# Hybrid decoder step in float32: how the first output tiles, the loads of x, the small loads and the output are ordered

## The chip, the cores and the metric

The kernel runs on one core of a Trainium2 chip. The metric is the device time of one execution in microseconds (us), lower is better. Three executions of the kernel before took 1625.08, 1626.22 and 1627.49 us; the median is 1626.22 us.

## The reference

One trunk layer of a hybrid decoder over 320 tokens (256 of a prompt and 8 sequences of 8), with 2048 channels, all in float32:

```python
hn = rms_norm(x, lp['norm_mix'])
proj = hn @ lp['w_in']                       # 2048 -> 6656 = 52 tiles of 128 columns
p_rw, p_hg, p_lru = jnp.split(proj, (RWKV_COLS, RWKV_COLS + HGRN_COLS), axis=-1)
y_rw, ... = rwkv7_mix(p_rw, ...)             # 12 heads of 64, delta rule
y_hg, ... = hgrn2_mix(p_hg, ...)             # 6 heads, 128 x 128 state
y_lru, ... = rglru_mix(p_lru, ...)           # 512 channels
x = x + concat([y_rw, y_hg, y_lru]) @ lp['w_out']
hn = rms_norm(x, lp['norm_ffn'])
gte, val = jnp.split(hn @ lp['ffn_w_up'], 2, axis=-1)
gc, ... = causal_dwconv(gte, ...)
x = x + (silu(gc) * val) @ lp['ffn_w_down']  # d_ff = 5632
```

After it stands a final RMSNorm. Outputs are the two parts of y and all recurrent states.

## The kernel before, in words

Activations lie transposed: 16 row blocks of 128 channels by 320 tokens. To keep float32 accuracy, TensorE multiplies split operands. ScalarE rounds a weight chunk to a high part `wh` (L173) and VectorE subtracts to get the low part `wl` (L174); x is split likewise into `xh` and `xl` (L217, L218), already scaled by the norm's weights `nmix`. An output tile of 128 columns then takes 16 row blocks times three products (`wh·xh`, `wh·xl`, `wl·xh`), 48 matmuls with 320 columns each. The RMS factor `rstd` is applied after the product, when VectorE evicts the accumulator.

Weights come in chunks of eight row blocks (128 x 1024 floats, 512 KB), so an input tile has two chunks. The order of all chunks stands in the list `chunks` (L97 on). SP issues their loads. `prefetch` (L176) keeps at most four chunks loaded and two split ahead of the one in use. There are three buffers each for `raw`, `wh` and `wl`.

**The first stage (L256 to L317).** Three products of a zero tile (`idle`, L260) run while the first loads are under way. In four groups g of four row blocks, SP is given half a chunk of tile 0, four loads of x of 160 KB each (L278) and half a chunk of tile 1; ScalarE and VectorE split them in that order. The squares of x for the norm are computed on ScalarE and added on VectorE into `ssq` beside that. `nmix` has its own small load on ScalarE's queue (L263), and `prm` and `cst` are loaded from there in groups 1 and 2. GpSimd issues the small loads `shift`, `h0` and `ccv` (L322 to L326) at the start. `first_tiles` (L300) multiplies, for each g, four row blocks of tile 0 and then of tile 1, into two PSUM banks of `aux_r`.

**The front (L395 to L418).** Then the third tile (k of head pair 0, `ps_k`) runs through `gemm` (L189), which takes one of two accumulators (`acc`). After it stands the product of `ones` with `ssq` (L401), which gives the sum of squares; ScalarE takes the root (L234) and VectorE the reciprocal (L235). The masks are loaded (L405) behind other work on SP's queue. Tiles 0 and 1 are evicted by `shifted` (L372), which also needs `shift`; they become `lora` and `sg`, the inputs of the low-rank products of every RWKV pair.

**The mixing stage (L1187 to L1198)** goes through `ORDER`: pair 0 of RWKV, HGRN head 0, pair 1, head 1 and so on, then the gated recurrences. A pair has tiles k, r, v; a head q, f, v, g. In `rwkv_pair(0, ps_k)` the tiles r and v are computed, v into a bank of `aux_r`. So the accumulators go to k, r, then q of head 0 and f of head 0, in turn.

The recurrences' own instructions are put between the tiles by a planner written in Python. `state["clock"]` counts 0.136 for every matmul of a tile (`GEMM_COST`) and 0.4 for every step of a recurrence (`AUX_COST`). Each of six queues (`QUEUES`, one for RWKV operands "f", one for RWKV chunks "r", and so on) holds jobs, one of which is active at a time. A step that ends in `yield w` is due again when the clock has gone on by w. `tick` runs what is due; it is called after every 4 row blocks of the `wh` products and at the end of a chunk, so three times per chunk. For pair 0, `rwkv_operands` (L474) yields `L_FIRST` before its first products (L482, the low-rank products with `lora`); after them come the square of k (L499) and its product (L502). `rwkv_chunks` (L563) waits for v and the operands. Its job for pair 1 begins when that of pair 0 has ended. A pair ends in `rwkv_norm` with L842 and L844. `y_steps` (L1176) splits the mixed outputs in turn once all six pairs are done; the output projection starts when eight of them are split (L1198), and reads x again (L1207).

**The end (L1281 to L1292).** After the last tile of the MLP's down projection, the sum of squares, a root and a reciprocal, VectorE scales 16 tiles one after the other (L1289, L1291), and each is stored by a DMA of its own, in turn on SP's and ScalarE's queues.

The order of instructions within an engine is otherwise chosen at build time by the framework's scheduler; `tc.keep_in_program_order` holds an instruction at its place in the text. `behind` (L185) is such a load on SP.

Of the kernel before, what the change touches and what calls it, by code (L numbers as in the profile page):

```python
# [66 lines left out]
def kernel(ctx: ExitStack, tc: tile.TileContext, i: dict, o: dict):  # L67
# [30 lines left out]
    for h in range(2):  # L98
        for n in range(2):
            chunks.append((i["w_in"][n, h], 8))  # L100
    for n in [c for k, m in ORDER for c in
                       {"r": (3 + 3 * m, 2 + 3 * m, 4 + 3 * m), "h": range(20 + 4 * m, 24 + 4 * m),
                        "l": (44 + 4 * m, 46 + 4 * m, 45 + 4 * m, 47 + 4 * m)}[k]]:
        for h in range(2):
            chunks.append((i["w_in"][n, h], 8))
# [83 lines left out]
    def gemm(pieces, xh, xl, k0=0, first=True, last=True, ps=None):  # L189
        if ps is None:  # L190
            ps = acc_p.tile([P, 512], F32, tag="acc", name="acc")
        for c, kc in enumerate(pieces):
            prefetch()
            wh, wl = splits.pop(state["used"])
            state["used"] += 1
            for k in range(kc):
                st = first and c == 0 and k == 0
                PE.matmul(ps[:, :T], wh[:, k, :], xh[k0 + k], start=st, stop=False)  # L198
                PE.matmul(ps[:, :T], wh[:, k, :], xl[k0 + k], start=False, stop=False)  # L199
                state["clock"] += 2 * GEMM_COST  # L200
                if k % 4 == 3:
                    tick()
            for k in range(kc):
                en = last and c == len(pieces) - 1 and k == kc - 1
                PE.matmul(ps[:, :T], wl[:, k, :], xh[k0 + k], start=False, stop=en)  # L205
# [77 lines left out]
    for g in range(4):  # L283
        ks = slice(4 * g % 8, 4 * g % 8 + 4)
        split_weights(2 * (g // 2), ks)
# [5 lines left out]
        split_weights(2 * (g // 2) + 1, ks)  # L291
        if g:
            squares(range(4 * g - 4, 4 * g) if g < 3 else ())
        if g == 1:
            tc.keep_in_program_order(S.dma_start(out=prm, in_=i["prm"]))
        if g == 2:
            tc.keep_in_program_order(S.dma_start(out=cst, in_=i["cst"]))
    state["raw"] = state["split"] = 4

    def first_tiles():  # L300

        pss = [aux_r(), aux_r()]
        for g in range(4):
            for n, ps in enumerate(pss):
                wh, wl = splits[2 * (g // 2) + n]
                for k in range(4 * g, 4 * g + 4):
                    PE.matmul(ps[:, :T], wh[:, k % 8, :], xh[k], start=(k == 0), stop=False)
                    PE.matmul(ps[:, :T], wh[:, k % 8, :], xl[k], start=False, stop=False)
                for k in range(4 * g, 4 * g + 4):
                    PE.matmul(ps[:, :T], wl[:, k % 8, :], xh[k], start=False, stop=(k == NK - 1))  # L310
            state["clock"] += 24 * GEMM_COST
            if g % 2:
                for n in range(2):
# [81 lines left out]
    def rwkv_front():  # L395
        ps_0, ps_1 = first_tiles()
# [4 lines left out]
        tc.keep_in_program_order(PE.matmul(ps_n[:, :T], ones, ssq, start=True, stop=True))  # L401
# [16 lines left out]
        return ps_k  # L418
# [41 lines left out]
    def rwkv_pair(p, ps_k=None):  # L460
# [5 lines left out]
        for name, n in (("k", 3), ("r", 2), ("v", 4)):  # L466
            ps = gemm(W_CHUNKS, xh, xl, ps=aux_r()) if p == 0 and name == "v" else ps_k
            ps_k = None
# [5 lines left out]
    def rwkv_operands(p, lw, box):  # L474
# [6 lines left out]
        for n, ps in enumerate((ps_w, ps_a)):  # L481
            PE.matmul(ps[:, :T], lw[half[n], n, :], lora[half[n], :], start=True, stop=True)  # L482
# [338 lines left out]
    def rwkv_norm(p, lw, y, bo):  # L821
# [21 lines left out]
        yo = yp.tile([P, T], F32, tag=f"y{p}", name="yo")  # L843
# [33 lines left out]
    def hgrn_steps(n, box):  # L877
# [148 lines left out]
        yo = yp.tile([P, T], F32, tag=f"y{NPAIR + n}", name="yo")  # L1026
# [77 lines left out]
    def lru_steps(m, box):  # L1104
        tiles = (2 * m, 2 * m + 1)
        rs, ths, aes = [], [], []
        for n, (xc, _) in zip(tiles, box["x"]):
            w = rp.tile([P, 2, P], F32, tag="wg", name="wg", bufs=1)
            G.dma_start(out=w, in_=i["wg"][n])
# [35 lines left out]
        for j, (n, hs) in enumerate(zip(tiles, rs)):  # L1145
# [4 lines left out]
            yo = yp.tile([P, T], F32, tag=f"y{NPAIR + NHG + n}", name="yo")  # L1150
# [36 lines left out]
    ps_k = rwkv_front()  # L1187
    spawn("y", y_steps())
    for kind, n in ORDER:
# [4 lines left out]
        if (kind, n) == ("r", 0):  # L1194
            rwkv_pair(0, ps_k)
# [9 lines left out]
    def x2_tile(n, ps):  # L1205
        t = yp.tile([P, T], F32, tag=f"y{n}", name="x2")
        G.dma_start(out=t, in_=i["xT"][n])  # L1207
# [78 lines left out]
    for n in range(NK):  # L1286
# [5 lines left out]
        (S if n % 2 else SY).dma_start(out=o["yT"][n], in_=y)  # L1292
# [5 lines left out]
L_FIRST = 11.0  # L1298
# [23 lines left out]
NFIRST = 4  # L1322
QUEUES = "nrfhly"
# [3 lines left out]
    "yT": (NK, P, T), "p_rwkv": (NPAIR, P, 64), "s_rwkv": (NPAIR, P, SB, 64), "nshift": (P, 20, 9),  # L1327
# [141 lines left out]
```

## Time and profile before

| what | value |
|---|---|
| median of three executions | 1626.22 us |
| the profiled execution | 1627.56 us |
| its span on the chip | 1625.8 us |
| busy share of PE / DVE / ACT / POOL | 99% / 60% / 50% / 9% |
| bytes moved by DMA | 238.91 MB, 147 GB/s on the mean |

In the profile, PE is TensorE, DVE VectorE, ACT ScalarE and POOL GpSimd; SP only issues DMAs. A row of the timeline gives the start and the duration in us, the engine, the line, the operation, the tiles (out<-in), the shape, a count, and in brackets how long the engine had been idle before and what released it. A matmul's duration overlaps with its neighbour's, so the rate is read from the starts. A row of the windows view gives, for a stretch of the span, its length, then for each engine the busy time and in brackets the number of instructions, then the granted TensorE clock, the DMA engines' busy share and GB/s.

### The profile page before, as it was taken

What the parts mean: (1) busy time and instruction counts of PE and PEld (TensorE: products, weight loads), DVE (VectorE), ACT (ScalarE), POOL (GpSimd) and SP (SyncE); (2) the same over time, 40 slices, a digit from 0 to 9 for tenths busy, and PEclk for the clock granted to TensorE, in tenths of its full rate; (3) what the DMA queues carried; (4) which work ended last, traced back from release to release, by engine and by line L of the source; (5) the groups of instructions that cost most, each with busy time, mean ns of one, the idle gap of its engine ahead of it and who ended that gap; (6) DMA issues with size and microseconds to landing.
All of it is one profiled execution on the core that took longest, in us unless ns stands there. A gap on an engine that the chain in (4) does not pass through costs nothing.

```text
span 1625.8 us, 29013 instructions
## 1 busy us (share of the span) xinstructions
PE 1601.6 (99%) x11478; PEld 1548.6 (95%) x11478; DVE 973.9 (60%) x1965; ACT 809.6 (50%) x1280; POOL 144.7 (9%) x364
## 2 busy tenths in 40 slices
PE   9999999999999999999999999999999999999996
PEld 8888989898989999999999999999999999999996
DVE  7786878777776765555555554343455555554444
ACT  7766766676766964443434343323334343344442
POOL 2101111111111300001111110000011110000000
PEclk9999999999999999999999999999999999999998
DMA  8444343444344554454445444555444444445553
GB/s 266 154 132 135 117 141 120 128 120 136 114 135 122 168 169 150 151 158 148 151 148 156 145 153 144 147 152 149 155 151 154 146 153 145 155 146 156 149 151 109
DMA packets 87791, 238.91 MB, mean 147 GB/s; under 512 B 16712, under 2 KB 31096, under 8 KB 87656
## 3 DMA queue, kind: packets, MB, share of 16 engines
q1 hardware_dynamic: 81496, 221.01, 44.4%
q0 software_dynamic: 4576, 14.16, 2.6%
q8 instruction: 90, 1.47, 0.4%
q10 hardware_dynamic: 1584, 1.89, 0.3%
q14 instruction: 45, 0.37, 0.1%
HBM read 225.66 MB, written 11.37 MB: 146 GB/s over the span
## 4 chain that ended last, share of the span: by engine, by line
PE 85%; ACT 7%; DVE 4%; DMA 2%; issue 2%; SPq 0%; POOL 0%; DVEq 0%; ACTq 0%
PE acc L198 26%; PE acc L205 26%; PE acc L199 26%; DVE wl L174 1%; PE aux_r L703 1%; PE aux_h L914 1%; ACT wh L173 1%; DMA raw<-in_w_in 1%; ACT L935 0%; ACT L893 0%; ACT L1023 0%; DVE x L1289 0%; PE aux_r L656 0%; PE aux_r L729 0%; DMA mskf<-in_msk 0%
## 5 line engine op out<-in xcount | busy, mean ns | idle before, releaser
L173 ACT CAST wh<-raw 128x1024 fp32r<-128x1024 f32 (+2 forms) x412 | 421.6, 1025 | 542.8 <-PE acc L199 338.2
L198 PE MATMUL acc<-xh,wh 128*128 128x320 f32 x2192 | 661.0, 315 | 0.0
L199 PE MATMUL acc<-xl,wh 128*128 128x320 f32 x2192 | 648.2, 309 | 0.0
L174 DVE TENSOR_TENSOR wl<-raw,wh 128x1024 fp32r<-128x1024 f32 (+2 forms) x412 | 489.9, 1190 | 224.5 <-ACT wh L173 113.1
L198 PEld LDWEIGHTS acc<-xh,wh 128*128 128x128 f32 x2192 | 411.7, 188 | 13.6 <-issue 10.7
L199 PEld LDWEIGHTS acc<-xl,wh 128*128 128x128 f32 x2192 | 411.7, 188 | 1.3
L205 PE MATMUL acc<-xh,wl 128*128 128x320 f32 x2192 | 372.6, 312 | 0.0
L205 PEld LDWEIGHTS acc<-xh,wl 128*128 128x128 f32 x2192 | 332.3, 188 | 2.8
L198 PE MATMUL acc<-hh,wh 128*128 128x320 f32 x704 | 207.9, 308 | 0.0
L199 PE MATMUL acc<-hl,wh 128*128 128x320 f32 x704 | 207.9, 308 | 0.0
L199 PEld LDWEIGHTS acc<-hl,wh 128*128 128x128 f32 x704 | 132.1, 188 | 0.0
L198 PEld LDWEIGHTS acc<-hh,wh 128*128 128x128 f32 x704 | 131.7, 187 | 0.0
L205 PE MATMUL acc<-hh,wl 128*128 128x320 f32 x704 | 118.8, 308 | 0.0
L1251 POOL COPY ncch<-fe 128x18 f32<-128x18 f32 x44 | 49.7, 1131 | 652.7 <-DVE fe L1250 652.7
L205 PEld LDWEIGHTS acc<-hh,wl 128*128 128x128 f32 x704 | 107.1, 187 | 0.0
L1261 DVE TENSOR_TENSOR fv<-acc,rstd 128x320 f32<-128x320 f32 x44 | 21.6, 492 | 98.5 <-PE acc L205 98.5
L1249 DVE TENSOR_TENSOR fe<-acc,rstd 128x256 f32<-128x256 f32 x44 | 18.7, 425 | 99.6 <-PE acc L205 99.6
L214 ACT CAST hh<-fv 128x320 fp32r<-128x320 f32 x44 | 20.3, 460 | 96.9 <-DVE fv L1263 96.9
L198 PE MATMUL acc<-yhl,wh 128*128 128x320 f32 x224 | 66.2, 310 | 0.0
L199 PE MATMUL acc<-yhl,wh 128*128 128x320 f32 x224 | 66.0, 307 | 0.0
L1256 DVE SCALAR_TENSOR_TENSOR fc<-fe,prm,fc 128x336 f32<-128x336 f32 x88 | 49.8, 566 | 1.6
L1254 ACT ACTIVATE fc<-fe,prm 128x336 f32<-128x336 f32 x44 | 29.4, 669 | 35.7 <-DVE fe L1250 35.7
(416 smaller groups left out, 1616.6 us busy)
## 6 DMA issues: line engine op xcount, KB each, us to landing
raw<-in_w_up SPq DMA_DIRECT2D x176, 512.0 KB, 3.5
raw<-in_w_in SPq DMA_DIRECT2D x100, 512.0 KB, 3.5
raw<-in_w_dn SPq DMA_DIRECT2D x64, 512.0 KB, 3.4
raw<-in_w_out SPq DMA_DIRECT2D x32, 512.0 KB, 3.6
raw<-in_w_dn SPq DMA_DIRECT2D x32, 384.0 KB, 3.0
out_s_hgrn<-hs POOLq DMA_DIRECT2D x12, 256.0 KB, 4.6
xr<-in_xT SPq DMA_DIRECT2D x16, 160.0 KB, 3.8
hs<-in_hs POOLq DMA_DIRECT2D x10, 256.0 KB, 4.2
```

The lines of the kernel that those rows point to most:

```text
L173: S.copy(wh[:, ks, :], raws[n][:, ks, :])
L174: V.tensor_tensor(wl[:, ks, :], raws[n][:, ks, :], wh[:, ks, :].bitcast(F32), op=ALU.subtract)
L198: PE.matmul(ps[:, :T], wh[:, k, :], xh[k0 + k], start=st, stop=False)
L199: PE.matmul(ps[:, :T], wh[:, k, :], xl[k0 + k], start=False, stop=False)
L205: PE.matmul(ps[:, :T], wl[:, k, :], xh[k0 + k], start=False, stop=en)
L214: S.copy(xh, src)
L703: PE.matmul(ps[q, b * 64:(b + 1) * 64], lhs[q, b, q], r[q], start=True, stop=True)
L1249: V.tensor_tensor(e[:, 2:258], ps[:, 0:TP], rstd[:, 0:TP], op=ALU.mult)
L1251: G.tensor_copy(ncch[:, j], e[:, 248:EX].rearrange("p (b s) -> p b s", s=10)[:, :, 8:10])
L1254: S.activation(c[:, 0:N], e[:, 0:N], AF.Identity, scale=pc("fw", 3 * j), bias=pc("fb", j))
L1256: V.scalar_tensor_tensor(c[:, 0:N], e[:, m:m + N], pc("fw", 3 * j + m), c[:, 0:N], op0=ALU.mult, op1=ALU.add)
L1261: V.tensor_tensor(val, ps[:, :T], rstd, op=ALU.mult)
```

## The change

Six edits:

- The first stage computes three tiles in turn instead of two: tiles 0, 1 and 3 (`FIRST_TILES`; tile 3 is k of pair 0). For each group of four row blocks, tile 0, 1 and 3 get 12 matmuls each. k goes into an accumulator. In the mixing stage's order, tile 3 is left out of `chunks`.
- After the first two matmuls of tile 0, two zero products (`NIDLE2`) are issued on TensorE.
- x is loaded in pairs of row blocks (320 KB); row block 0 comes together with `nmix` in one load `x0`, row block 1 in a load of its own. All row blocks lie in one tile `yall`, which is also where the mixed outputs, the second residual and the final output lie.
- Small loads move: `shift`, `h0`, `ccv` and the first `wg` from GpSimd's queue to SP's, at later places; `cst` and `prm` behind all splits of the first stage, still on ScalarE's queue.
- The front computes r of pair 0 before `rwkv_pair(0)` is entered, and the product with `ssq` stands within r's last chunk, ahead of its `wl` products. The low-rank products of pair 0 are held at their place, and `L_FIRST` goes from 11 to 15.
- The output is stored in pairs of tiles, eight DMAs of 320 KB in turn on SP's and ScalarE's queues.

```diff
     for h in range(2):
-        for n in range(2):
+        for n in FIRST_TILES:
             chunks.append((i["w_in"][n, h], 8))
...
-    def gemm(pieces, xh, xl, k0=0, first=True, last=True, ps=None):
+    def gemm(pieces, xh, xl, k0=0, first=True, last=True, ps=None, within=None):
...
+            if within and c == len(pieces) - 1:
+                within()
             for k in range(kc):
                 en = last and c == len(pieces) - 1 and k == kc - 1
                 PE.matmul(ps[:, :T], wl[:, k, :], xh[k0 + k], start=False, stop=en)
...
-    nmix = cp.tile([P, NK], F32, tag="nmix", name="nmix")
-    S.dma_start(out=nmix, in_=i["prm"][:, PRM["nmix"]:PRM["nmix"] + NK])
-    xh, xl, xr = [], [], []
+
+    x0 = et("diff", NK + T)
+    nmix = x0[:, 0:NK]
+    yall = yp.tile([P, NK, T], F32, tag="yall", name="yall")
+    xh, xl = [], []
...
-    raws[3] = rp.tile([P, 10, P], F32, tag="big", name="raw3", bufs=BB)
+    NF = len(FIRST_TILES)
+    for n in (NF, NF + 1):
+        raws[n] = rp.tile([P, 10, P], F32, tag="big", name=f"raw{n}", bufs=BB)
     for g in range(4):
         ks = slice(4 * g % 8, 4 * g % 8 + 4)
-        if g < 3:
-            load(2 * (g // 2), ks)
-        for k in range(4 * g, 4 * g + 4):
-            t = yp.tile([P, T], F32, tag=f"y{k}", name="xr")
-            SY.dma_start(out=t, in_=i["xT"][k])
-            xr.append(t)
-        if g == 3:
-            load(2, ks)
-        load(2 * (g // 2) + 1, ks)
+        first = NF * (g // 2)
+        load(first, ks)
+        if g == 0:
+            SY.dma_start(out=x0, in_=i["x0"])
+            SY.dma_start(out=yall[:, 1, :], in_=i["xP"][0, :, 1, :])
+        for m in range(2 * g, 2 * g + 2):
+            if m:
+                SY.dma_start(out=yall[:, 2 * m:2 * m + 2, :], in_=i["xP"][m])
+        for n in range(1, NF):
+            load(first + n, ks)
...
-        split_weights(2 * (g // 2) + 1, ks)
-        if g:
-            squares(range(4 * g - 4, 4 * g) if g < 3 else ())
-        if g == 1:
-            tc.keep_in_program_order(S.dma_start(out=prm, in_=i["prm"]))
-        if g == 2:
-            tc.keep_in_program_order(S.dma_start(out=cst, in_=i["cst"]))
-    state["raw"] = state["split"] = 4
+        for n in range(1, NF):
+            split_weights(first + n, ks)
+        if g in (1, 2):
+            squares(range(4 * g - 4, 4 * g))
+    tc.keep_in_program_order(S.dma_start(out=cst, in_=i["cst"]))
+    tc.keep_in_program_order(S.dma_start(out=prm, in_=i["prm"]))
+    state["raw"] = state["split"] = 2 * NF
...
-        pss = [aux_r(), aux_r()]
+        pss = [aux_r(), aux_r(), acc_p.tile([P, 512], F32, tag="acc", name="acc")]
...
                     PE.matmul(ps[:, :T], wh[:, k % 8, :], xl[k], start=False, stop=False)
+                    if n == 0 and k == 0:
+                        for _ in range(NIDLE2):
+                            tc.keep_in_program_order(PE.matmul(ps_i[:, :T], idle[:, 0:P], idle, start=True, stop=True))
...
-    G.dma_start(out=shift, in_=i["shift"])
...
-    G.dma_start(out=h0, in_=i["h0"])
...
-    G.dma_start(out=ccv, in_=i["ccv"])
...
-        ps_k = gemm(W_CHUNKS, xh, xl)
+        behind(out=shift, in_=i["shift"])
         ps_n = aux_h()
-        tc.keep_in_program_order(PE.matmul(ps_n[:, :T], ones, ssq, start=True, stop=True))
+        ps_r = gemm(W_CHUNKS, xh, xl, within=lambda: tc.keep_in_program_order(
+            PE.matmul(ps_n[:, :T], ones, ssq, start=True, stop=True)))
...
+        behind(out=h0, in_=i["h0"])
+        behind(out=ccv, in_=i["ccv"])
...
-            PE.matmul(ps[:, :T], lw[half[n], n, :], lora[half[n], :], start=True, stop=True)
+            pin = tc.keep_in_program_order if p == 0 else lambda ins: ins
+            pin(PE.matmul(ps[:, :T], lw[half[n], n, :], lora[half[n], :], start=True, stop=True))
...
-            G.dma_start(out=w, in_=i["wg"][n])
+            (behind if n == 0 else G.dma_start)(out=w, in_=i["wg"][n])
...
-        (S if n % 2 else SY).dma_start(out=o["yT"][n], in_=y)
+        if n % 2:
+            (S if n % 4 == 3 else SY).dma_start(out=o["yP"][n // 2], in_=yall[:, n - 1:n + 1, :])
...
-L_FIRST = 11.0
+NIDLE2 = 2
+L_FIRST = 15.0
...
+FIRST_TILES = (0, 1, 3)
```

More of the change, by code (lines that the diff above doesn't have):

```diff
@@ L102 @@
                        {"r": (3 + 3 * m, 2 + 3 * m, 4 + 3 * m), "h": range(20 + 4 * m, 24 + 4 * m),
-                        "l": (44 + 4 * m, 46 + 4 * m, 45 + 4 * m, 47 + 4 * m)}[k]]:
+                        "l": (44 + 4 * m, 46 + 4 * m, 45 + 4 * m, 47 + 4 * m)}[k] if c not in FIRST_TILES]:
         for h in range(2):
@@ L269, in squares @@
             add_square(ssq, xr[k], k, lambda: rp.tile([P, T], F32, tag="c", name="sq", bufs=BC))
[L271 removed]
+    NF = len(FIRST_TILES)
+    for n in (NF, NF + 1):
+        raws[n] = rp.tile([P, 10, P], F32, tag="big", name=f"raw{n}", bufs=BB)
     for g in range(4):
         ks = slice(4 * g % 8, 4 * g % 8 + 4)
[L274 to L282 removed]
+        first = NF * (g // 2)
[8 more added lines that the diff above has]
+            load(first + n, ks)
+    xr = [yall[:, k, :] if k else x0[:, NK:NK + T] for k in range(NK)]
     for g in range(4):
         ks = slice(4 * g % 8, 4 * g % 8 + 4)
[L285 removed]
+        first = NF * (g // 2)
+        split_weights(first, ks)
         for k in range(4 * g, 4 * g + 4):
@@ L308, in first_tiles @@
                     PE.matmul(ps[:, :T], wh[:, k % 8, :], xl[k], start=False, stop=False)
+                    if n == 0 and k == 0:
+                        for _ in range(NIDLE2):
+                            tc.keep_in_program_order(PE.matmul(ps_i[:, :T], idle[:, 0:P], idle, start=True, stop=True))
                 for k in range(4 * g, 4 * g + 4):
                     PE.matmul(ps[:, :T], wl[:, k % 8, :], xh[k], start=False, stop=(k == NK - 1))
-            state["clock"] += 24 * GEMM_COST
+            state["clock"] += 12 * NF * GEMM_COST
             if g % 2:
-                for n in range(2):
+                for n in range(NF):
                     splits.pop(state["used"])
@@ L417, in rwkv_front @@
         free(xo)
-        return ps_k
+        return ps_k, ps_r
     STEP = 16 * P + 16
@@ L466, in rwkv_pair @@
         for name, n in (("k", 3), ("r", 2), ("v", 4)):
-            ps = gemm(W_CHUNKS, xh, xl, ps=aux_r()) if p == 0 and name == "v" else ps_k
-            ps_k = None
+            if p:
+                ps = None
+            elif name == "k":
+                ps = ps_k
+            elif name == "r":
+                ps = ps_r
+            else:
+                ps = gemm(W_CHUNKS, xh, xl, ps=aux_r())
             box[name] = shifted(n + 3 * p, ps)
@@ L842, in rwkv_norm @@
         PE.matmul(ps_g[:, :T], lw[:, 2, :], sg, start=True, stop=True)
-        yo = yp.tile([P, T], F32, tag=f"y{p}", name="yo")
+        yo = yall[:, p, :]
         V.tensor_tensor(yo, ps_g[:, :T], bo, op=ALU.mult)
@@ L1025, in hgrn_steps @@
         V.tensor_tensor(rs, ps_o[:, :T], rs, op=ALU.mult)
-        yo = yp.tile([P, T], F32, tag=f"y{NPAIR + n}", name="yo")
+        yo = yall[:, NPAIR + n, :]
         V.scalar_tensor_tensor(yo, rs, pc("hnw", n), g, op0=ALU.mult, op1=ALU.mult)
@@ L1149, in lru_steps @@
             S.activation(gt, gt, AF.Gelu_apprx_tanh)
-            yo = yp.tile([P, T], F32, tag=f"y{NPAIR + NHG + n}", name="yo")
+            yo = yall[:, NPAIR + NHG + n, :]
             hp, hs_ = extended(hs)
@@ L1185, in y_steps @@
             yield L_Y
-    ps_k = rwkv_front()
+    ps_k, ps_r = rwkv_front()
     spawn("y", y_steps())
@@ L1205, in x2_tile @@
     def x2_tile(n, ps):
-        t = yp.tile([P, T], F32, tag=f"y{n}", name="x2")
-        G.dma_start(out=t, in_=i["xT"][n])
+        t = yall[:, n, :]
+        G.dma_start(out=t, in_=i["xP"][n // 2, :, n % 2, :])
         V.tensor_tensor(t, ps[:, :T], t, op=ALU.add)
@@ L1326 @@
 _OUTS = {
-    "yT": (NK, P, T), "p_rwkv": (NPAIR, P, 64), "s_rwkv": (NPAIR, P, SB, 64), "nshift": (P, 20, 9),
+    "yP": (NK // 2, P, 2, T), "p_rwkv": (NPAIR, P, 64), "s_rwkv": (NPAIR, P, SB, 64), "nshift": (P, 20, 9),
     "p_hgrn": (NHG, P, P), "s_hgrn": (NHG, P, SB, P), "nh": (P, NLRU, 9), "nccv": (P, NLRU, 9, 3),
@@ L1430 @@
     arrays = {
-        "xT": x.T.reshape(NK, P, T),
+        "xP": x.T.reshape(NK // 2, 2, P, T).transpose(0, 2, 1, 3),
+        "x0": np.concatenate([prm["nmix"], x.T[0:P]], axis=1),
         "w_in": chunked(w_in), "w_out": chunked(w_out), "w_up": w_up, "w_dn": w_dn,
```

10 lines of the change are left out of this document (5 added, 5 removed).

## The prediction

> **What bounds the kernel.** I read the page first, then the windows view stage by stage, then the timeline of TensorE where it idles.
>
> ```profile
> span 1625.8 us, 29013 instructions
> PE 1601.6 (99%) x11478; PEld 1548.6 (95%) x11478; DVE 973.9 (60%) x1965; ACT 809.6 (50%) x1280; POOL 144.7 (9%) x364
> ```
> ```profile
> 0.00:20.00 20.00, 17.17 (x79) 14.26 (x79) 13.76 (x32) 14.74 (x32) 5.52 (x23) 1.00 0.91 299
> ...
> 800.00:1200.00 400.00, 400.00 (x2729) 400.00 (x2728) 196.22 (x274) 145.89 (x171) 24.66 (x54) 1.00 0.49 150
> ```
>
> TensorE bounds it. In the MLP 2729 matmuls take 400 us, 0.1466 us each and 7.04 us for an output tile of 48; nothing there is touched. The first 20 us hold fewer products, with the DMA engines at 0.91. So the change can win only what TensorE loses in the first 100 us. The profiled execution took 1627.56 us, 1.76 above its span and 1.34 above the median of 1626.22; I subtract my sum from the median.
>
> ```profile
> 1.38 3.57 PE L260 MATMUL aux_h<-idle 128*128 128x320 f32 x6 [1.38 <-DVE idle L257]
> 4.70 0.63 PE L307 MATMUL aux_r<-xh,wh 128*128 128x320 f32 x1
> 5.43 0.63 PE L308 MATMUL aux_r<-xl,wh 128*128 128x320 f32 x1
> 7.18 0.64 PE L307 MATMUL aux_r<-xh,wh 128*128 128x320 f32 x1 [1.12 <-ACT xh L217]
> ...
> 8.47 0.47 PE L308 MATMUL aux_r<-xl,wh 128*128 128x320 f32 x1
> 8.73 0.47 PE L307 MATMUL aux_r<-xh,wh 128*128 128x320 f32 x1
> ...
> 10.57 0.31 PE L308 MATMUL aux_r<-xl,wh 128*128 128x320 f32 x1
> 10.71 0.32 PE L307 MATMUL aux_r<-xh,wh 128*128 128x320 f32 x1
> ```
> ```profile
> 6.57 1.47 ACT L217 ACTIVATE xh<-xr,nmix 128x320 fp32r<-128x320 f32 x3 [1.55 <-DMA xr<-in_xT]
> ...
> 18.49 0.62 ACT L173 CAST wh<-raw 128x512 fp32r<-128x512 f32 x1 [1.63 <-DMA raw<-in_w_in]
> ```
>
> Three losses show. TensorE waits 1.12 us for the second row block of x. Until about 10.5 us products start 0.26 us apart, then 0.14 (the windows row says 1.00 for the granted clock all the same, so I go by the starts). And at 18.49 ScalarE has waited 1.63 us for half a weight chunk: with two tiles in turn, four row blocks of x and two half chunks (1.18 MB) must come for 24 products (3.5 us).
>
> ```profile
> 24.17 0.31 PE L198 MATMUL acc<-xh,wh 128*128 128x320 f32 x1
> ...
> 30.04 1.33 PE L205 MATMUL acc<-xh,wl 128*128 128x320 f32 x8
> 32.22 0.81 PE L401 MATMUL aux_h<-ext,cst 128*128 128x320 f32 x2 [0.85 <-DVE ext L253]
> ...
> 47.77 0.41 PE L198 MATMUL acc<-xh,wh 128*128 128x320 f32 x1
> ...
> 50.07 0.31 PE L199 MATMUL acc<-xl,wh 128*128 128x320 f32 x1
> 51.57 0.81 PE L502 MATMUL aux_r<-kn,cst 128*128 128x320 f32 x2 [1.19 <-ACT kn L499]
> ```
> ```profile
> 97.41 0.66 PE L686 MATMUL aux_r<-cst,U 128*128 128x128 f32 x4 [0.99 <-DMA U<-du]
> ```
>
> The third tile ends at 30.04 + 8 x 0.1466 = 31.21. Then come 1.01 us until the sum of squares (L401), 1.35 before L502 (50.22 to 51.57) and 0.99 before L686.
>
> **Part by part. Three tiles in turn.** A group is now 36 products, 5.28 us, and asks for 1.44 MB.
>
> ```profile
> 11.87 1.13 ACT L173 CAST wh<-raw 128x512 fp32r<-128x512 f32 x2
> ...
> 12.91 1.92 ACT L217 ACTIVATE xh<-xr,nmix 128x320 fp32r<-128x320 f32 x4
> ...
> 15.32 1.55 ACT L252 ACTIVATE sq<-xr 128x320 f32<-128x320 f32 x4
> ```
> ```profile
> 12.82 1.29 DVE L174 TENSOR_TENSOR wl<-raw,wh 128x512 fp32r<-128x512 f32 x2
> ...
> 14.03 1.93 DVE L218 SCALAR_TENSOR_TENSOR xl<-xr,nmix,xh 128x320 fp32r<-128x320 f32 x4
> ...
> 16.48 2.27 DVE L253 TENSOR_TENSOR ext<-ext,sq 128x320 f32<-128x320 f32 x4
> ```
>
> VectorE needs 1.5 x 1.29 + 1.93 = 3.9 us a group, and 2.27 more in the two groups that add squares: 20.0 us over four, against 21.1 of TensorE. ScalarE needs less. The 5.8 MB of x and three tiles take 19.3 us at the 299 GB/s of the first window, and the last half chunk is wanted after 25. So TensorE is the bound, after the first group. Third and later tiles also reuse the three split buffers: the first split of group 2 waits for tile 0's last product of group 1. ScalarE then has the time of two tiles in a group (3.5 us) for one cast and four blocks (0.6 + 1.9), so this costs nothing unless VectorE is behind.
>
> **First gap.** The first product still waits for the first half chunk, 4.70. The second ends at 6.06. The zero products are four passes of at most 0.6 us (six took 3.57), so 2.4 us if the clock is slow throughout, 1.2 if it is fast; I take 1.7, as some lie on either side of the turn. They hide the wait for row block 1. The remaining 142 products take 20.8: the third tile ends at 6.06 + 1.7 + 20.8 = 28.6 instead of 31.2, **a gain of 2.6**. At best the zeros take 1.2: 3.1. At worst they take 2.4 and products stay 0.26 apart until 10.5, 2 us at 56% of speed, 0.9 more: 1.0.
> In the Trainium skill, the page "TensorE: Matmul & The Clock Gate" (Part 1) says that half clock lasts until a window of about 3.4 us was busy throughout, and that the windows run free of the kernel's start. The trace agrees as far as 3.3 us of dense work from 7.18 to the turn. By that rule unbroken work from 1.38 would turn the clock between 4.8 and 8.2, which lies nearer my best end than my worst.
>
> **Small loads.** `shift`, `h0`, `ccv`, `nmix`, `prm` and `cst` leave the busy first 20 us; the gain is counted above. On SP they stand in front of weight chunks, behind the masks; two more issues of about 0.5 us. Nobody waits for them before the eviction of tile 0. Zero to -0.3; I take zero.
>
> **Sum of squares inside r.** The last eight squares get 40 products of r (5.9 us) of cover, where they were 1.0 late: **+1.0** (0 if VectorE is behind).
>
> **Accumulator of k.** Now it is a wait that appears.
>
> ```profile
> 33.63 2.15 DVE L235 RECIPROCAL rstd<-rstd_s 128x320 f32<-128x320 f32 x1 [0.32 <-ACT rstd_s L234]
> ...
> 39.32 0.42 DVE L378 TENSOR_TENSOR ext<-aux_r,rstd 128x256 f32<-128x256 f32 x1 [0.48 <-POOL nshift L381]
> 41.93 0.43 DVE L378 TENSOR_TENSOR ext<-acc,rstd 128x256 f32<-128x256 f32 x1
> ```
>
> From L401's end (33.0) over the reciprocal and the evictions of tiles 0 and 1 to the eviction of k's accumulator (42.6) pass 9.6 us. The tile q of head 0 needs that accumulator, at 47.77, 5 us later. After the change q comes 8 products and the tile v after the sum of squares: 1.2 + 7.0 = 8.2 us. TensorE would wait 9.6 - 8.2 = 1.4, less what GpSimd's masks cost (0.48), more if two weight subtractions fall in between: **-1.0** (0 to -2.4).
>
> **`L_FIRST`, r before the spawn.** Worked out with the planner's due times: before, L482 came due 1.09 + 0.4 + 11 = 12.5 units after r's start and ran at v's end (13.5), two tiles on. Now the job starts at r's end and is due 16.5 later; v ends at 6.9, q at 13.5, the first chunk of f at 16.7: 3.5 tiles after r's start. L502 follows a third of a tile later as before, but without the masks in SP's way of weights: I take half of its wait, **+0.7** (0 to 1.35). L686 gets 1.6 units more after its DMA chain is begun: **+0.5** (0 to 1.0).
>
> The chunk jobs follow each other, so all six pairs come 1.5 tiles later, by the same stepping: their first products at 5.5, 12.5, ... 40.5 tiles instead of 4.0, 11.0, ... 39.0, the last L842 at 47.8 instead of 46.5 of 49.
>
> ```profile
> 549.86 0.70 PE L842 MATMUL aux_r<-sg,lw 128*128 128x320 f32 x2
> ...
> 567.75 0.31 PE L198 MATMUL acc<-yhl,wh 128*128 128x320 f32 x1
> ```
> ```profile
> 559.13 0.48 DVE L215 TENSOR_TENSOR yhl<-yo,yhl 128x320 fp32r<-128x320 f32 x1
> ```
>
> The last pair's output is split at 559.6 and wanted at 567.75 + 10 x 0.1466 = 569.2, 9.6 us of room for a delay of 9.4 to 10.6: **-0.3** (0 to -1.0).
>
> ```profile
> 240.00:400.00 160.00, 158.82 (x1294) 143.52 (x1294) 121.12 (x346) 106.94 (x212) 19.67 (x50) 1.00 0.41 126
> 400.00:600.00 200.00, 198.05 (x1522) 183.97 (x1521) 146.36 (x371) 143.23 (x269) 30.62 (x79) 1.00 0.45 140
> ```
>
> The mixing stage idles 3.1 us in these 360. Pairs and heads now meet in another phase; I take 0, with 1.5 either way.
>
> **Output in pairs.**
>
> ```profile
> 1616.11 6.12 DVE L1289 TENSOR_TENSOR x<-x,rstd 128x320 f32<-128x320 f32 x15
> 1622.15 0.55 DVE L1291 SCALAR_TENSOR_TENSOR x<-x,prm,rstd 128x320 f32<-128x320 f32 x1
> ```
> ```profile
> GB/s 0 0 0 0 0 0 0 0 0 0 0 0 0 0 0 0 0 0 96 371 375 400 394 384 394 391 387 394 381 400 387 384 397 381 397 243 0 0 0 0
> ```
>
> VectorE makes 160 KB in 0.41 us, the stores move it at 390 GB/s, 0.42 us. The last store carries twice as much, 0.42 us more after the last tile, against the backlog that the earlier ones leave now: **-0.1** (-0.4 to +0.3).
> The page "DMA: Bandwidth & Descriptors" of the Trainium skill (Rules for kernel authors) would have transfers of 1 MiB and more for full bandwidth, so pairs should gain; the stores of 160 KB here already run at 371 to 400 GB/s.
>
> **Sum:** 2.6 + 1.0 - 1.0 + 0.7 + 0.5 - 0.3 - 0.1 = 3.4 us. 1626.2 - 3.4 = **1622.8 us**.
>
> **Rivals.**
> - *The accumulator's wait eats it* (chance 0.20). For it: 9.6 against 8.2. It costs 2.4, and the late operands leave L502 waiting: 3.4 - 1.4 - 0.5 = 1.5, 1624.7 us.
> - *Neither wait appears* (0.20). For it: the scheduler may put k's eviction first, and L502 and L686 get more cover: 2.6 + 1.0 + 1.35 + 1.0 = 6.0, 1620.3 us.
> - *The zero products do not do what they are for* (0.08): the clock turns at 10.5 as before and they only stand in the way; 1.6 less, 1624.4 us.
> - *The pairs' delay reaches the output projection* (0.07), slower. The place is the split of pair 5's output; it decides once the delay passes the 9.6 us of room. At 2.5 tiles (17.6 us) TensorE stands 8.0 us: 3.4 + 0.3 - 8.0 = -4.3, 1630.5 us. For it: each job starts where the last ended, so nothing catches up. Against it: the due times give 1.3 to 1.5 tiles.
>
> **Numbers.** What is left, 0.45, is the forecast. About 0.2% (3.25 us) can be told from no change; the forecast lies 0.15 beyond that, so I count 0.29 of it and 0.19 of the second rival as faster: 0.48. Slower 0.07, the rest 0.45. The range runs from a bit below the second rival, 1619.0, to 1626.5, which takes in the first and third with the mixing stage's 1.5; it leaves out the slow rival and the tails.
>
> **What would show it.** Zero products between the second and third product and spacing of 0.147 from about 8 us; third tile ended at 28 to 29.5; no idle time before the sum of squares; a wait of about 1 us at q's first product on VectorE's eviction; L482 in the middle of f. I am wrong if TensorE waits in group 2 or 3 for splits, if the mixing stage's idle time grows by over 2 us, or if the split of pair 5 is what the output projection waits for.

## The result and the profile after

The changed kernel is slower. Four executions took 1641.13 to 1649.57 us, median 1643.97, against 1625.79 before (1625.08 to 1627.49): a ratio of 1.0115, 95% interval 1.0087 to 1.0142, some 18 us. The profiled execution took 1644.14 us.

The head of its page, to be read against the one of before (1625.8 us; PE 1601.6, ACT 809.6 x1280):

```profile
span 1642.4 us, 28931 instructions
PE 1605.6 (98%) x11482; PEld 1554.2 (95%) x11482; DVE 975.0 (59%) x1967; ACT 832.6 (51%) x1299; POOL 158.4 (10%) x360
```

The span is 16.6 us longer: TensorE is busy 4.0 us more, with four small passes of zeros in it, and idle 12.6 us more. ScalarE is busy 23.0 us more in only 19 more instructions. ScalarE is not the bound engine, but the experiments below lead to these 23 us. The windows view says where TensorE idles, in its first pair of columns:

```profile
160.00:240.00 80.00, 77.30 (x618) 70.39 (x619) 59.99 (x189) 56.33 (x106) 13.30 (x25) 0.98 0.38 116
240.00:400.00 160.00, 154.59 (x1260) 140.28 (x1258) 116.96 (x336) 112.35 (x212) 24.84 (x48) 1.00 0.40 125
400.00:600.00 200.00, 192.51 (x1498) 175.51 (x1497) 146.12 (x389) 147.75 (x281) 37.19 (x81) 1.00 0.41 125
```

From 240 to 600 us it idles 12.9 us where the kernel before idled 3.1. None of the products of that stage was edited. The head, which was edited, did about what it should. TensorE's timeline:

```profile
5.61 1.95 PE L319 MATMUL aux_h<-idle 128*128 128x320 f32 x4
...
29.30 0.31 PE L198 MATMUL acc<-xh,wh 128*128 128x320 f32 x1
...
35.17 0.70 PE L410 MATMUL aux_h<-ext,cst 128*128 128x320 f32 x2
46.28 0.39 PE L198 MATMUL acc<-xh,wh 128*128 128x320 f32 x1 [2.20 <-DVE ext L388]
57.00 0.81 PE L500 MATMUL aux_r<-lora,lw 64*128 64x320 f32 x4
```

The first product of r, at 29.30, marks the end of the third tile: 1.9 us earlier than 31.21. No idle time stands before the sum of squares. The wait for k's accumulator came, 2.20 us. TensorE's waits in the first 640 us, with what released them (us in total, times, longest):

```profile
PE aux_r L500 <- ACT bkt L660: 7.5, 4, 1.9
PE aux_h L1034 <- DVE oi L1023: 2.3, 4, 0.6
PE acc L198 <- DVE ext L388: 2.2, 1, 2.2
PE aux_h L979 <- DVE qk L972: 1.9, 1, 1.9
PE aux_r L649 <- DVE mt L602: 1.7, 1, 1.7
```

The largest is new and regular, once in each of four pairs: the low-rank products (L500) of the next pair wait for ScalarE's copies of `bkt`. One such place, on TensorE and then on ScalarE:

```profile
164.13 0.81 PE L658 MATMUL aux_r<-cst,BK 64*128 64x64 f32 x8
...
169.81 1.08 PE L500 MATMUL aux_r<-lora,lw 64*128 64x320 f32 x4 [1.88 <-ACT bkt L660]
```
```profile
162.61 1.28 ACT L852 ACT_TABLE_LOAD   x1
163.91 0.53 ACT L852 ACTIVATE sqy<-aux_r,eps_t 128x320 f32<-128x320 f32 x1
164.33 0.20 ACT L650 COPY vs<-aux_r 128x64 f32<-128x64 f32 x1
164.55 1.28 ACT L853 ACT_TABLE_LOAD   x1
165.85 0.47 ACT L853 ACTIVATE sqy<-sqy 128x320 f32<-128x320 f32 x1
...
167.20 1.28 ACT L1027 ACT_TABLE_LOAD   x1
168.49 0.47 ACT L1027 ACTIVATE hg<-hg 128x320 f32<-128x320 f32 x1
168.87 0.64 ACT L856 ACTIVATE yc<-yc,prm 128x320 f32<-128x320 f32 x1
169.41 0.62 ACT L660 COPY bkt<-aux_r 128x256 f32<-128x256 f32 x2
```

The transposes of BK fill two of the four banks of `aux_r` at 164.13. L500 needs two banks and gets them only when ScalarE has copied `bkt` out, in copies that start at 169.41. Ahead of them in ScalarE's order, from 162.61 on, stand three loads of its function tables (`ACT_TABLE_LOAD`), 3.85 us. Two belong to the norm of the pair before (L852 the logarithm, L853 the exponential). In the kernel before the same two operations (L834, L835) stand here:

```profile
147.53 1.28 ACT L893 ACT_TABLE_LOAD   x1
148.82 0.56 ACT L893 ACTIVATE b<-b,eps_t 128x320 f32<-128x320 f32 x1
149.29 0.35 ACT L623 COPY vsw<-aux_r 128x256 f32<-128x256 f32 x1
149.54 0.53 ACT L834 ACTIVATE sqy<-aux_r,eps_t 128x320 f32<-128x320 f32 x1
150.09 1.28 ACT L935 ACT_TABLE_LOAD   x1
...
152.35 0.46 ACT L835 ACTIVATE sqy<-sqy 128x320 f32<-128x320 f32 x1
```

There the norm's logarithm comes right behind the logarithm of the HGRN head (L893), its exponential right behind the head's exponentials (L935), and both find their tables loaded. ScalarE's groups say the same for the whole run: after, both lines load a table in all six pairs, before in one. In all it is 95 loads after and 78 before; 17 x 1.283 = 21.8 us of the 23.0.

```profile
L852 ACT ACT_TABLE_LOAD x6 | 7.7, 1283 | 0.1
L853 ACT ACT_TABLE_LOAD x6 | 7.7, 1283 | 0.1
```
```profile
L834 ACT ACT_TABLE_LOAD x1 | 1.3, 1283 | 0.0
L835 ACT ACT_TABLE_LOAD x1 | 1.3, 1283 | 0.0
```

### The profile page after: what moved, and what is told of

Same layout as the page of the kernel before. It is cut to its first block, busy times and chain, and to the rows that moved or that the text cites. A ratio compares the mean times of both kernels' runs of the same rounds, so it can differ in the third digit from the quotient of the medians.

```text
span 1642.4 us, 28931 instructions
## 1 busy us (share of the span) xinstructions
PE 1605.6 (98%) x11482; PEld 1554.2 (95%) x11482; DVE 975.0 (59%) x1967; ACT 832.6 (51%) x1299; POOL 158.4 (10%) x360
## 3 DMA queue, kind: packets, MB, share of 16 engines
q10 hardware_dynamic: 864, 1.88, 0.3%
## 4 chain that ended last, share of the span: by engine, by line
PE 86%; ACT 8%; DVE 3%; issue 2%; DMA 1%; POOL 0%; SPq 0%; DVEq 0%; ACTq 0%
PE acc L198 26%; PE acc L199 26%; PE acc L207 25%; ACT wh L173 1%; PE aux_h L932 1%; PE aux_r L721 1%; ACT L853 0%; ACT L522 0%; DVE wl L174 0%; ACT L852 0%; ACT L1027 0%; PE aux_r L674 0%; DVE yall L1307 0%; DMA raw<-in_w_in 0%; DMA mskf<-in_msk 0%
## 5 line engine op out<-in xcount | busy, mean ns | idle before, releaser
L207 PE MATMUL acc<-xh,wl 128*128 128x320 f32 x2176 | 371.5, 312 | 0.0
L207 PEld LDWEIGHTS acc<-xh,wl 128*128 128x128 f32 x2176 | 329.6, 188 | 4.4 <-issue 1.2
L207 PE MATMUL acc<-hh,wl 128*128 128x320 f32 x704 | 118.8, 308 | 0.0
L207 PEld LDWEIGHTS acc<-hh,wl 128*128 128x128 f32 x704 | 107.1, 187 | 0.0
```

## The experiments

Two theories stood at the start. **Phase**: `L_FIRST` and the later spawn put the pairs' steps 1.5 tiles later against the HGRN heads, and this alone costs the time. **Front**: the accumulator for k, r ahead of the spawn or the moved loads cost it, whatever the phase. Each run names its median and its ratio to the kernel before with the interval.

**The phase put back.** Changed kernel, one constant:

```diff
-L_FIRST = 15.0
+L_FIRST = 5.0
```


> The changed kernel with L_FIRST = 5 in place of 15: nothing else differs. By the due times the low-rank products of pair 0 then run 2.0 tiles after r's start and the chunk products of the pairs at 4.0, 11.0, ... 39.0 tiles, as in the kernel before, instead of 5.5, 12.5, ... 40.5. Theory (the 1.5 tiles put each pair's chunk steps onto the low-rank products of the next pair, which then wait for PSUM banks behind ScalarE): the waits at L500 behind ScalarE's copies (7.5 us in all) and the clock drops after them go, and the time comes to 1622 to 1627 us, since the head's gain of 1.9 us stays. Rival (the loss comes from k in an accumulator, the loads moved to SP, or r ahead of the spawn, whatever the phase): 1638 to 1644 us.

1627.45 us, ratio 1.0004 (0.9995 to 1.0014): 16.5 us less than the change. There are 78 table loads and no wait of L500 for `bkt`. But the head's 1.9 us do not show in the time. What stood in their way is below.

**The phase alone, in the kernel before:**

```diff
-L_FIRST = 11.0
+L_FIRST = 21.0
```


> The kernel before with L_FIRST = 21 in place of 11, nothing else of the change: its pairs then run 1.5 tiles later, chunk products at 5.5, 12.5, ... 40.5 tiles. Theory (phase alone): slower by 12 to 20 us, 1638 to 1646 us, with waits of the low-rank products (L482) behind ScalarE's copies of bkt (L642). Rival (another edit is the cause): 1625 to 1629 us.

1643.88 us, ratio 1.0106 (1.0090 to 1.0121), 95 table loads, and the waits of L482 for `bkt` are 7.5 us in 4 times again. One constant reproduces the loss without any of the other edits. Front is refuted as its main cause.

**Low-rank products moved away.** The changed kernel with

```diff
-        if p == 0:
-            yield L_FIRST
+        yield L_FIRST if p == 0 else L_LOW      # L_LOW = 10.0
```


> The changed kernel, L_FIRST = 15, in which the low-rank products of pairs 1 to 5 are due 10 units (1.5 tiles) later, so that they no longer fall between the transposes of BK and ScalarE's copies of them; the chunk steps stay where the change put them. Theory: the 7.5 us of waits at L500 and the slow clock behind them go, 1630 to 1636 us, the rest of the loss (waits on HGRN's steps and the like, some 8 us) stays. Rival (it is the chunk steps against the HGRN head's and ScalarE's other work, and the low-rank products only show it): under 3 us of gain, 1640 to 1644 us, with the waits found at another line.

1643.98 us, ratio 1.0110 (1.0095 to 1.0125): no gain. L500 waits no more, but the next to need a bank does (waits of TensorE):

```profile
PE aux_r L673 <- ACT bkt L659: 6.4, 5, 1.3
PE aux_h L1033 <- DVE oi L1022: 6.2, 4, 1.6
```

So the meeting of L500 with the banks is not the cause. What is left is that ScalarE is late and whoever comes next waits; the run without the loads, below, tests that.

**The constant of before, left at 11:**

```diff
-L_FIRST = 15.0
+L_FIRST = 11.0
```


> The changed kernel with L_FIRST left at 11, as the kernel before has it: chunk products at 5.0, 12.0, ... 40.0 tiles, 1.0 later than before instead of 1.5; the low-rank products of the next pair then come after the transposes of AR (L691) instead of between those of BK and their copies. Theory of the bank wait: the wait is set by what stands just ahead of L500, so it nearly goes: 1624 to 1632 us. Rival (the delay itself costs, about 10 us a tile): 1632 to 1637 us.

1632.95 us, ratio 1.0042 (1.0027 to 1.0057), with 91 table loads: the rival's range. L500 waits no longer and 6 us are lost all the same, so the bank wait at L500 cannot be the whole story.

**Only the table loads taken away.** Changed kernel, `L_FIRST` = 15:

```diff
-        S.activation(lnv, ps_v[:, :T], AF.Ln, scale=1.0 / 64, bias=eps_ln)
-        S.activation(lnv, lnv, AF.Exp, scale=-0.5)
+        S.activation(lnv, ps_v[:, :T], AF.Identity, scale=1.0 / 64, bias=eps_ln)
+        S.activation(lnv, lnv, AF.Identity, scale=-0.5)
```


> The changed kernel, L_FIRST = 15, with the logarithm and the exponential of the RWKV pair's norm replaced by two Identity operations of the same size (so the norm's root is left out): the order of TensorE and of ScalarE stays the same but for 12 table loads of 1.28 us that are gone. Theory (the two table loads ahead of ScalarE's copies of bkt hold the PSUM banks that the next low-rank products need): the waits at L500 behind bkt (7.5 us) and the slow clock behind them go, 1628 to 1635 us. Rival (the banks themselves, or the chunk steps against VectorE's work): 1640 to 1645 us.

1629.55 us, ratio 1.0019 (1.0010 to 1.0029): 14.4 us less than the change. TensorE's 11482 products stand in the same order in both profiles, and ScalarE's instructions differ by the twelve loads and the order of a few around the last pair. So the two profiles can be laid side by side, product by product: from 14 to 160 us they are level to 0.1 us. Then the changed kernel falls behind by 4.2 us at the wait shown above, with the slow clock after it, by some 2.6 us at each of the next three (near 252, 334 and 416 us), by 1.9 near 498 and by 1.2 at 594, and nowhere else by more than 0.1. The wait of L500 is gone from the list. The windows, against those above:

```profile
160.00:240.00 80.00, 79.26 (x649) 72.16 (x650) 63.81 (x197) 54.73 (x108) 13.29 (x25) 1.00 0.41 128
240.00:400.00 160.00, 158.50 (x1297) 144.05 (x1295) 121.47 (x351) 109.00 (x213) 26.61 (x50) 1.00 0.40 126
400.00:600.00 200.00, 196.98 (x1528) 181.87 (x1527) 147.23 (x381) 145.27 (x278) 35.96 (x80) 1.00 0.44 137
```

Twelve loads, 15.4 us on an engine that is busy half of the time, cost 14.4 us of the whole. The control is the same edit in the good phase (in the kernel with k in `aux_r`, below):

> The run with k in aux_r, L_FIRST = 5, with the same replacement (the norm's root is left out). The control for the run that took 12 table loads out of the changed kernel: theory (in this phase the norm's two operations share their tables with the HGRN head's and hold nobody): within 1 us of 1627.25. Rival (the replacement is a gain by itself, whatever the phase): 5 us or more less.

1626.93 us, ratio 1.0003 (0.9994 to 1.0013), against 1627.25 without the edit. There the replacement gains nothing, so the 14.4 us are the loads at those places.

**Two more phases.** Changed kernel with `L_FIRST` = 7, and the last of the mended kernels below with 6 in place of 5:

> The changed kernel with L_FIRST = 7: chunk products at 4.33, 11.33, ... tiles, a third of a tile later than in the kernel before, and lw long there when the low-rank products of pair 0 come. ScalarE has 88 table loads in this order, against 78 with L_FIRST = 5 and 95 with 15. Theory (what costs is ScalarE's table loads at the place where the two streams meet): 1626 to 1634 us in spite of the lw wait gone. Rival (only the delay in tiles counts, 10 us a tile): 1622 to 1626 us.

1646.49 us, ratio 1.0124 (1.0109 to 1.0140): worse than either theory said, at a third of a tile from the good phase. The largest wait is `L816 <- DVE gbd L784`, 8.1 us in 4 times. It has 88 table loads; what part of its loss is theirs was not tested.

> As the run with single stores, with L_FIRST = 6 instead of 5: the chunk steps come at most a sixth of a tile later, and ScalarE still has 78 table loads, while L_FIRST = 7 had 88 and took 1646 us. Theory (table loads count, not the delay): within 1 us of the run with L_FIRST = 5. Rival (any delay costs 6 to 10 us a tile): 1 to 3 us more.

1636.05 us, ratio 1.0055 (1.0042 to 1.0068), some 8.5 us more than with 5, with the same 78 table loads. My theory that only table loads count fell here. TensorE's waits in it:

```profile
PE aux_r L724 <- DVE T L716: 4.7, 5, 0.9
PE aux_r L802 <- DVE sbd L815: 4.4, 5, 0.9
PE aux_r L668 <- ACT uv L655: 2.5, 5, 0.5
PE aux_r L846 <- DVE y L831: 2.5, 1, 2.5
```

By these waits they are steps within a pair that now come too soon after the ones whose results they need. With the norm's two operations replaced as before:

> The run with L_FIRST = 6 (1636.05 us, 78 table loads, waits at L724, L802, L668, L846 of 14 us in all), with the logarithm and exponential of the pair's norm replaced by Identity (the norm's root is left out), which takes 2 table loads away. Theory (there the loss comes from steps that stand a sixth of a tile too close to the results they need, not from table loads): 1633 to 1637 us. Rival (table loads at a bad place, even where their number is no larger): 1626 to 1630 us.

1632.37 us, ratio 1.0036 (1.0022 to 1.0050), a little below the first expectation. The four waits stay as they are (4.7, 4.4, 2.4, 2.5), and from 160 to 600 us TensorE is busy 428.4 us with the replacement and 428.3 without. So in this phase it is not table loads that cost the time in the mixing stage, but these waits. The 3.7 us between the medians are mostly the clock's, as far as the profiles tell. TensorE's products stand in the same order in both, and of the 3.9 us between the profiles 2.0 arise near 96 us and 1.3 near 554. At both places the profile without the replacement has 3.4 us of half clock behind a wait (1.89 and 2.47 us), and the other has none, though its waits are nearly as long (1.46 and 2.48). The one execution of the five at a mean clock of 0.997, which all four of the run with the replacement have, took 1633.33 us.

**Where the head's gain went.** With `L_FIRST` = 5 alone, one wait of TensorE and what the clock did after it (last columns: clock, DMA share, GB/s):

```profile
45.69 1.53 PE L500 MATMUL aux_r<-lora,lw 64*128 64x320 f32 x4 [2.16 <-DMA lw<-in_lw]
```
```profile
46.00:48.00 2.00, 2.00 (x7) 1.14 (x7) 0.71 (x1) 1.78 (x5) 0.76 (x1) 0.50 0.99 379
48.00:50.00 2.00, 2.00 (x10) 2.00 (x9) 1.89 (x5) 1.85 (x5) 0.60 (x2) 0.50 0.81 315
50.00:52.00 2.00, 2.00 (x8) 1.91 (x8) 0.00 (x0) 1.97 (x4) 0.19 (x1) 0.50 0.01 2
```

`lw` is loaded when the pair is entered, which the change puts behind r. Loaded earlier (`rwkv_pair` then takes `lw0` for pair 0 in place of a load of its own; `L_FIRST` is 5 in this run and in those of the changed kernel that follow):

```diff
         behind(out=shift, in_=i["shift"])
+        lw0 = rp.tile([P, 3, P], F32, tag="lw", name="lw", bufs=2)
+        behind(out=lw0, in_=i["lw"][0])
```


> The changed kernel with L_FIRST = 5 and one edit more: the load of lw of pair 0 is issued behind shift, about 14 us earlier. With L_FIRST = 5 alone TensorE stood 2.16 us at the low-rank products of pair 0 for lw, and ran the next 7.5 us at half clock. Theory (the head's gain is there and was lost at this wait): wait and slow clock go, 5 to 6 us less, unless the first product of q now waits for the accumulator of k (up to 2.5 us, with a slow clock behind it): 1621 to 1626 us. Rival (the first 40 us gain nothing that lasts): 1626 to 1628 us, as with L_FIRST = 5 alone.

1629.28 us, ratio 1.0017 (1.0008 to 1.0026): not less but 1.8 us more. The wait moved to the accumulator of k, and half clock follows again until 55 us:

```profile
48.66 0.61 PE L198 MATMUL acc<-xh,wh 128*128 128x320 f32 x1 [3.37 <-DVE ext L388]
```

So k was given a bank of its own, beside the early `lw`:

```diff
-        pss = [aux_r(), aux_r(), acc_p.tile([P, 512], F32, tag="acc", name="acc")]
+        pss = [aux_r(), aux_r(), aux_r()]
```


> As the run with the early lw, and k of pair 0 goes into a bank of aux_r in place of an accumulator, so that the first product of q need not wait for the eviction of k. Theory: no wait of over 0.5 us before 60 us, the whole gain of the head stays (1.9 us by the third tile, 1.0 at the sum of squares, about 1 at L520): 1620 to 1624 us. Rival (the wait for k's accumulator does not occur with this phase): the same time as with the early lw alone, within 1 us.

1627.25 us, ratio 1.0007 (0.9998 to 1.0016). Both waits are gone and the clock stays at 1.00, 2.0 us less than the run before it. But it is no faster than the kernel before. VectorE shows new slack in it:

```profile
29.26 0.49 DVE L255 TENSOR_TENSOR ext<-ext,sq 128x320 f32<-128x320 f32 x1
...
36.23 2.15 DVE L237 RECIPROCAL rstd<-rstd_s 128x320 f32<-128x320 f32 x1 [2.57 <-ACT rstd_s L236]
```

The last square is added by 29.75 us, but the product that sums them stands in r's second chunk, at 34.53, so the reciprocal starts 2.6 us later than before the change (33.63). All evictions hang on it. Moved to the first chunk:

```diff
-            if within and c == len(pieces) - 1:
+            if within and c == 0:
```


> As the run with k in aux_r, and the product of ones with ssq stands in r's first chunk instead of its second, 3.5 us earlier. In that run ssq was complete at 29.75 us and its product ran at 34.53; VectorE then stood 2.57 us before the reciprocal, which began at 36.23 against 33.63 in the kernel before, and TensorE waited 1.12 us for kn and 1.65 us for the products with the masks. Theory (the late product delays VectorE's whole chain by what the head gained): reciprocal at about 32.7 us, both waits under 0.5 us, 2 to 3 us less, 1624 to 1625.5 us. Rival (VectorE is late for other reasons): within 0.7 us of 1627.2.

1627.76 us, ratio 1.0009 (1.0000 to 1.0017): the reciprocal starts at 33.41 as it should, the time does not move. TensorE waits for kn (1.84 us) and at two more places instead:

```profile
PE aux_r L523 <- ACT kn L520: 1.8, 1, 1.8
...
PE aux_r L707 <- DMA U<-du: 1.0, 1, 1.0
PE aux_r L652 <- DVE mt L605: 0.9, 1, 0.9
PE acc L207 <- DVE wl L174: 0.9, 1, 0.9
```

TensorE is 2.2 us ahead of the kernel before when L523 ends its wait (49.40 against 51.57), and level with it at pair 1's chunk products (143.93 against 144.01). Between these it waits for VectorE, 0.9 us each at L652 and L207. In the run before, its one profile was still 2.3 us ahead at that point (141.70). But that execution took 1626.38 us, near the fastest of its eleven, and the profiled execution of the kernel before, 1627.56 us, is slower than all four that are given with the result. A lead of 2.3 us between two single profiles is no more than executions differ by, so it is not shown that the head's gain lasts.

**The output.** The kernel above with single stores, first into the new layout, then (k in `aux_r`, sum of squares as in the change) into blocks as before:

```diff
-        if n % 2:
-            (S if n % 4 == 3 else SY).dma_start(out=o["yP"][n // 2], in_=yall[:, n - 1:n + 1, :])
+        (S if n % 2 else SY).dma_start(out=o["yP"][n // 2, :, n % 2, :], in_=y)   # second run: out=o["yT"][n]
```


> As the run before this one, and the output is stored tile by tile as in the kernel before, 16 stores in turn on two queues. In four kernels with stores in pairs the span ends 3.57 to 3.63 us after VectorE's last operation, in the kernel before 3.1. Theory (the last pair of 320 KB costs 0.5 us): 0.5 us less than with pairs, 3.0 to 3.2 after VectorE's last operation. Rival (the difference is the load of the queues): no difference.

1627.59 us, ratio 1.0005 (0.9996 to 1.0014); the span ends 3.85 us after VectorE's last operation, against 3.59 with pairs and 3.1 in the kernel before.

> The run with k in aux_r, and the output is stored as in the kernel before: 16 single stores, each to a block of 160 KB of its own (the run with single stores wrote into the interleaved layout of pairs, at 353 GB/s). Theory (pairs cost 0.5 us at the end): the span ends 3.0 to 3.2 us after VectorE's last operation, the time is 1626.7 us, 0.5 less than with pairs. Rival (the one tile yall as the source costs it): 3.6, no change.

1627.10 us, ratio 1.0001 (0.9993 to 1.0010); 3.85 us again, so single stores do not bring the 3.1 back. What both runs have in common is that the 16 tiles lie in the one tile `yall`. From there single stores move at some 355 GB/s, where they moved at 390 from tiles of their own, in as many packets (2304), and pairs at 390. Why the place of the source should matter no run shows.

```profile
GB/s 0 0 0 0 0 0 0 315 351 359 356 351 361 351 356 361 353 353 359 351 356 313 0 0 0 0 0 0 0 0 0 0 0 0 0 0 0 0 0 0
```
```profile
GB/s 0 0 0 0 0 0 0 0 236 389 394 405 369 394 389 405 389 374 394 399 394 312 0 0 0 0 0 0 0 0 0 0 0 0 0 0 0 0 0 0
```

The first row is of single stores into blocks, the second of pairs, both from `yall`.

**The zero products.** The run with single stores, without them, and the kernel before with nothing but them:

```diff
-NIDLE2 = 2
+NIDLE2 = 0
```


> As the run with single stores, without the zero products in the first gap (NIDLE2 = 0). Theory (they turn the clock early, as the third tile's end at 28.7 to 29.3 us against 31.2 shows): products stay 0.26 us apart until about 10 us, the third tile ends about 1 us later, 0.5 to 1.5 us more than with them. Rival (three tiles in turn do it alone): within 0.3 us.

1628.61 us, ratio 1.0011 (1.0002 to 1.0019), 1.0 us more than with them. The third tile ends at 30.87 instead of 29.36.

```diff
                     PE.matmul(ps[:, :T], wh[:, k % 8, :], xl[k], start=False, stop=False)
+                    if n == 0 and k == 0:
+                        for _ in range(2):
+                            tc.keep_in_program_order(PE.matmul(ps_i[:, :T], idle[:, 0:P], idle, start=True, stop=True))
```


> The kernel before with one part of the change alone: the two zero products (four passes) after the first two products of tile 0. Theory A (the zeros turn the clock early, 1.5 us by the third tile, but the sum of squares waits for VectorE, 0.85 us before, and takes it back): third tile ended at 29.5 to 30.3 us, the wait at L401 1.5 to 2.5 us, the time within 0.7 us of the kernel before. Theory B (the head's gain is kept while the order after it is untouched): 1.0 to 1.6 us less, 1625.0 to 1625.6 us.

1626.35 us, ratio 1.0000 (0.9991 to 1.0009). The third tile ends at 29.70 + 8 x 0.1466 = 30.87, 0.3 us earlier than without, less than both theories had assumed. So this run does not tell what a gain there would be worth. In these profiles three tiles alone gain 0.3 us by the third tile, the zeros alone 0.3, and both together 1.9. The timelines show why. With two tiles and the zeros, products stand 0.15 us apart from 9.4 us on, but the lead of 0.9 us shrinks to 0.65 by 12.7 us and to 0.4 at 19.2. There TensorE waits 0.45 us (before 0.24) for x, which ScalarE splits only behind a half chunk of weights that had come late, at 18.10. With three tiles and no zeros no such wait is left, but products stay 0.27 us apart until 13.2 us. That last time varies: the kernel before with `L_FIRST` = 21 has the same head as the kernel before, and there it is 13.1 instead of 10.5 and the third tile ends at 31.85, so 0.3 us is less than the same head differs by, and the late time without zeros may be chance. In the fourteen kernels with both, the third tile ended between 28.1 and 29.7 us.

No version was faster than the kernel before.

## Why the prediction was wrong

**The failed step** is the one sentence on the mixing stage: "Pairs and heads now meet in another phase; I take 0, with 1.5 either way." It measured some 17 us: 16.5 from the phase put back, and as much from the constant alone in the kernel before. In its place the runs show table loads: parted from the head's logarithm and exponential, the norm's two operations loaded a table each, and without these twelve loads 14.4 us were gone. One of the prediction's signs of being wrong came true, the mixing stage's idle time growing by over 2 us: it grew by 9.8 from 240 to 600 us. I had worked out the 1.5 tiles rightly (pair 0's chunk products stand at 5.5 tiles, pair 5's at 40.5), and asked only whether the last pair would be late. I did not ask what stands beside what within a period of seven tiles. The idle time of the mixing stage in the kernel before, 3.1 us of 360, was the result of one phase and said nothing of others; its bounds were drawn from nothing.

**The slow rival** had the right sign and the wrong place. The last pair's output was in time: the output projection began at 581.47 us without a wait, 13.7 us later than before (567.75). Of the rest of the 16.6 us between the spans, 1.9 were waits in its second tile for a weight chunk that ScalarE and VectorE had not split (at 594.74 and 598.09), and 0.5 the stores at the end. That "slower" had only 0.07 follows from having one slow mechanism in the list and none for the phase.

**Three tiles and first gap**, +2.6: 1.9 in the profile of the change, within the bounds. The zero products turn the clock early, as said, but that gains 1.9 us only together with the three tiles. The clock turned earlier: two products stood 0.14 us apart at 7.54 us, where they were 0.26 apart until 10.5.

**Sum of squares**, +1.0: the wait is gone, but moving its product behind r's first 40 products delayed VectorE's chain by 2.6 us or more (reciprocal at 36.23 in the mended kernel, 33.63 before). That price was missing. With the product in r's first chunk it is gone (33.41), but the time did not move (1627.76), so by this run the price was not what held the gain back.

**Accumulator of k**, -1.0 with bounds to -2.4: 2.20.

**L502 and L686**, +0.7 and +0.5: no idle stands before their counterparts (L520, L704) in the changed kernel, as everything in pair 0 came later. With the phase put back and k in `aux_r` the wait for kn is there again, 1.1 to 1.8 us.

**Output in pairs**, -0.1 with bounds to -0.4: it costs 0.5 us. The pairs move at the rate of before, so what is left to explain it is the last store of twice the size, which I had priced at 0.42 and then let a backlog take back. Single stores from `yall` do not show this apart, as they are slower by themselves.

**A sum.** The second rival's 6.0 leaves out the -0.3 and -0.1, which its condition does not touch: it comes to 5.6, 1620.6 us.

## What to carry to other kernels

When two streams of small steps are interleaved by due times, a delay that looks free at the end still changes which of their steps stand together. Before taking such a shift at nothing, list for one period what ScalarE does in the new order: here two operations that were parted from neighbours with the same function brought a table load of 1.28 us each, and these counted where a copy that frees a PSUM bank stood behind it. List, too, how far each step stands from the one whose result it needs: with `L_FIRST` = 6 some 8 us were lost with no table load more, at waits of that kind and the slow clock behind two waits. And a constant such as `L_FIRST` belongs to everything ahead of it: after any edit there, it has to be found again, in steps finer than a tile (here 5, 6 and 7 gave 1627, 1636 and 1646 us, the 6 in a slightly different kernel).

## What was unexpected in the hardware

Short waits of TensorE cost more than their length. After 2.16 us without a product (43.5 to 45.7) the granted clock was 0.50 from 45.4 to 52.3 us, 6.8 us at half speed. After the 1.88 us that end at 169.81 the changed kernel shows

```profile
167.47:170.88 3.41, 1.53 (x9) 0.83 (x7) 3.30 (x13) 3.38 (x7) 0.00 (x0) 1.00 0.17 23
170.88:174.29 3.41, 3.41 (x13) 3.03 (x12) 1.71 (x8) 3.37 (x6) 0.00 (x0) 0.50 0.34 131
```

while after the 2.20 us that end at 46.28 the clock stayed at 1.00. In these profiles there are seventeen slow stretches behind waits. Fifteen last 3.41 us and two last twice that, and in the 3.41 us ahead of each TensorE had stood idle for 47 to 80% (55% in the first row above). The 2.20 us are cut by such a grid: counted back from 170.88 in steps of 3.413 us, one stretch ends at 44.58 and the next, 50% idle, at 48.00. So what seems to count here is how much of one such stretch is idle, about half, and not the length of the wait alone. It is no sharp limit: in the run with `L_FIRST` = 6 and the norm's operations replaced, a stretch that is 55% idle (549.77 to 553.18) has no slow clock behind it.

The page "TensorE: Matmul & The Clock Gate" of the Trainium skill (Part 1) has the clock fall after an idle window of about 3.4 us, and its closing section (Why this matters for your kernels) warns of gaps over about 3. These traces disagree: gaps of 1.6 to 2.2 us were enough in some places and not in others. That the windows run free, as the page says, fits the difference between places.

The page "ScalarE: Activation LUTs" (Table sets) has a logarithm followed by an exponential cost one load, since one set holds both. Here L852 and L853, a logarithm and an exponential with only one copy or cast between them, loaded a table each, in all six pairs.
